# One load of attention values cut in two, and one spread of a bias row put three products later, in a fused decoder trunk on one core

## The chip, the cores and the metric

The kernel runs on one core of a Trainium2 chip. The metric is the device time of one execution in microseconds (us); the time of a kernel is the median of several executions. Beside it stands one execution that the hardware profiler recorded; its trace gives the span from the first to the last instruction and every row that is quoted below.

## The reference, cut to what matters

```python
mod = silu(c) @ w_ada + b_ada;  shift, scale, gate = split(mod, 3)
u = x * (1 + scale) + shift                       # 2048 x 1024
q, k, v, a_gate, p_in, p_gate, m_a, m_p = split(u @ w_in)
# 16 query heads of 64 on 2 key/value heads; window 128, blocks of 128 rows
logits = q_block @ [k_previous, k_own]^T / 8 + bias[head, distance]   # masked
probs  = softmax([logits, sink[head]])[..., :-1]
a = (probs @ [v_previous, v_own]) * silu(a_gate) @ w_attn_proj
p = (grouplinear(multiscale_pool(p_in)) * pool_scale * silu(p_gate)) @ w_pool_proj
y = ((sigmoid(m_a) * a + sigmoid(m_p) * p) @ w_out) * (1 + gate)
out = layer_norm(2**0.25 * x + y)
```

The eight query heads of one key/value head share its keys and values. The bias of a head depends on the distance between query and key alone, so a head's whole bias is one row of 384 numbers, read with a shift of one per query.

## The kernel before, in words

**The work.** The 2048 rows are taken in two chunks of 1024 (`s` = 0, 1), features in tiles of 128. All the large matrix products go through *quads* (class `Quad`): two 128-column weight tiles against two 512-row halves of a chunk, made as seven products after Strassen's and Winograd's scheme (B11, T1, T2, B21, T3, B22, T4). Each product is 12 matmuls of 128x128 by 512, because every operand is kept as a high and a low part and three of the four cross products are made. Weights of a quad arrive in tiles `W` and `A` (the last quarter), GpSimd (POOL) forms their sums and differences, ScalarE (ACT) and VectorE (DVE) split them into the parts `w_set`, TensorE (PE) multiplies.

**The order.** `plan` writes all products in one list, and `run` goes through it. `now[0]` is the number of the product that is made; `at(p, f)` hangs a function on product `p`, and `defer(n, f)` lets one run n products later. Each engine works through its own instructions in the order in which this walk emits them. Almost every DMA is issued by SyncE (SP, its queue SPq in the profile), so SP's order is a queue too: where one row waits (for data to be ready, for a buffer to be free, for an earlier transfer), all behind it wait. All operations are recorded by one helper, so nearly every row of the profile has line L56, and the tiles tell the rows apart.

**The overlay.** In each chunk a long phase (pools `o0` and `o1`) makes 13 quads one after the other and, between their matmuls, the attention of the same chunk (`overlay`, line 767). `beat` (line 940) is called after every third matmul and starts one attention step whenever enough credit has come together. There are 64 steps per chunk, each for two heads and one block of 128 queries; steps 0 to 31 are the first key/value group, 32 to 63 the second. In `step(n)` (line 871) PE makes the scores of block n into the one buffer `lg` (tiles `kk` and `qs`), the transposes of block n-2 (`pt`), and `values(n - 3)`, the product with the values (`pv<-pth,vv` and `pv<-ptl,vv`). DVE adds the bias `bt` to the scores and ACT makes the exponentials (tile `L`). PE takes its instructions in order, so when a step's operand is late, the large products behind it are late too.

**The values.** `load_v` (line 787) loads the values of one key/value group, 128 rows by 8 blocks of 128 numbers, into the tile `vv`, of which there is one. The second group's load is issued after step 34, the step that has made the last product with the first group's values, and its first reader, `values(32)`, is part of step 35; five calls of `beat` are skipped in between (`state[2] = 5`, line 955). For the second chunk the last block of the first chunk is loaded ahead of it with a DMA of its own. `values(32)` reads block 0 of `vv` in the first chunk, `values(33)` blocks 0 and 1, `values(34)` blocks 1 and 2.

**The bias.** `bias_rows` has written one row of 384 numbers per head to DRAM (`e_d`). `spread_bias(j, q)` (line 764) copies the rows of two heads to 128 places in the DRAM tile `e_rep` (384 KB), and `load_bias` (line 802) reads them back with a shift per partition into the tile `bt`, of which there is one; the load of the next two heads is issued in the last step of the present two. The eight spreads are hung on products: two early ones on ACT's queue, and j = 2 to 7 in the first overlay on SP's, at product `first + 10 * j - 17` (line 1443), with `first` the phase's first product. `e_rep` is one tile to the framework, so a spread waits until an earlier `bt` load has read it, though the rows are others.

**The query tiles.** The quads that make q store their result with two DMAs (`q_d<-q_hi`, `q_d<-q_lo`). The tiles `q_hi`, `q_lo`, `sig` and `px` share a ring of four buffers (tag `c`), so the third `q_hi` of a quad may be written when the store of its first one has landed.

Of the kernel before, what the change touches and what calls it, by code (L numbers as in the profile page):

```python
# [22 lines left out]
KT = D // P  # L23
CH = 512
NCH = S // CH
NB = CH // P
# [33 lines left out]
def kernel(  # L60
# [23 lines left out]
    pe, act, dve, pool, sp = (Ordered(tc, e) for e in (nc.tensor, nc.scalar, nc.vector, nc.gpsimd, nc.sync))  # L84
# [50 lines left out]
    v_d = dp.tile([2, P, 2, 2 * NB, P], F32, name="v_d")  # L135
# [11 lines left out]
    def as32(ap):  # L147
        return ap.bitcast(F32)
# [173 lines left out]
    def at(p, f):  # L322
        assert p >= now[0], (p, now[0])
        hooks.setdefault(int(p), []).append(f)
# [439 lines left out]
    def spread_bias(j, q):  # L764
        q.dma_start(e_rep[:, 2 * j : 2 * j + 2, :], e_d[2 * j : 2 * j + 2, :].partition_broadcast(P))

    def overlay(ph, s, n_slots):
# [19 lines left out]
        def load_v(kv):  # L787
            v = kvt["v"] = tp.tile([P, 2 * NB + s, P], F32R, tag="vv", bufs=1, name="vv")
            if s:
                sp.dma_start(as32(v[:, 0]), v_d[0, :, kv, 2 * NB - 1])  # L790
            sp.dma_start(as32(v[:, s:]), v_d[s, :, kv])

        def load_q(h):
            if h >= N // 2:
# [145 lines left out]
        def beat():  # L940
            n, credit, rest = state
            if rest:
                state[2] -= 1
                return
            state[1] += rate
            if state[1] >= 1 and n < N + 3:
                step(n)
                state[0] += 1
                state[1] -= 1
                if n == N // 2 - 1:  # L950
                    load_k(1)
                    state[2] = 8
                if n == N // 2 + 2:
                    load_v(1)
                    state[2] = 5
# [8 lines left out]
        load_q(0)  # L964
        load_bias(0)
        load_v(0)
        new_l(0)
        return beat, leave
# [34 lines left out]
    def input_sums(ph, first):  # L1003
        def load(u, k, at_c):
            sp.dma_start(u, xt[1, k].rearrange("p (h c) -> p h c", h=2)[:, :, at_c])

        def scale(u, k):
            act.activation(u, u, AF.Identity, bias=mod[:, k : k + 1], scale=mod[:, KT + k : KT + k + 1])

        for n in range(8):  # L1010
            steps(first, 1 + 11 * n, sums_job(ph, u1_d, n // 2, n % 2, load, scale))
# [424 lines left out]
    def middle(s):  # L1436
        def enter(ph, phase):
            first = phase["first"]
            beat, leave = overlay(ph, s, 4 * (phase["end"] - first))
            if s == 0:  # L1440
                input_sums(ph, first)
                for j in range(2, KT):
                    at(first + 10 * j - 17, lambda j=j: spread_bias(j, sp))
            return beat, leave

        return enter
# [120 lines left out]
```

## Time and profile before

| | us |
|---|---|
| median of 3 executions | 1715.49 |
| lowest and highest of them | 1715.05, 1715.85 |
| the profiled execution, its own time | 1721.38 |
| span of the profiled execution, first to last instruction | 1719.3 |

The profiled execution took 5.89 us more than the median, and 2.08 us of its time lie around the span. In rows of a timeline the columns are: start in us from the span's start, length in us, engine, line, operation, tile written <- tiles read, how many; in square brackets the time that the engine had been idle and what released it. SPq rows are the issue of a DMA, not its transfer; the transfer's end is called its landing. In rows that begin with a stretch (345.26:348.68) each engine has its busy time in the stretch and its number of instructions, then come the granted TensorE clock (1.00 is full), the mean busy share of the 16 DMA engines, and GB/s.

### The profile page before, as it was taken

Reading aid. Unit: us, or ns where it says so; the run is one execution under the profiler, and the core shown is the slowest. Engines: PE = TensorE matmul, PEld = TensorE weight load, DVE = VectorE, ACT = ScalarE, POOL = GpSimd, SP = SyncE. Lnnn points to the kernel's source line nnn. Section 1 sums busy time; section 2 is a strip of 40 time slices with the busy share of each in tenths; the row PEclk is TensorE's granted clock in tenths of the full one; section 3 lists DMA queues with packets and bytes.
Section 4 is the critical chain, followed back from the end, with each engine's and each line's share of the span. In section 5 each row is a group of like instructions: output and inputs, shape, how many; then the busy total and the mean of one; then the engine's idle time right before and its main releaser. Section 6 shows DMA issues by size and latency. Waiting matters only on the chain.

```text
span 1719.3 us, 24847 instructions
## 1 busy us (share of the span) xinstructions
PE 1672.1 (97%) x8112; PEld 1400.3 (81%) x8112; DVE 1274.5 (74%) x2295; ACT 945.4 (55%) x1815; POOL 590.5 (34%) x563
## 2 busy tenths in 40 slices
PE   9899999989999999999999999999999999999997
PEld 7678788878788888888888888888878888888886
DVE  5956787778756778658877888487886785778778
ACT  3644687767753436447777676433454443434552
POOL 3012455545553223323334243322243311113544
PEclk8999999999999999999999999999999999999999
DMA  9389666766547789873555544489978695778343
GB/s 355 120 285 301 204 213 228 244 214 201 190 162 228 254 281 316 285 249 119 183 178 188 180 145 154 160 268 325 336 260 290 199 331 182 259 261 295 147 147 122
DMA packets 236545, 389.50 MB, mean 227 GB/s; under 512 B 20840, under 2 KB 90240, under 8 KB 236288
## 3 DMA queue, kind: packets, MB, share of 16 engines
q1 hardware_dynamic: 235344, 386.55, 66.9%
q10 hardware_dynamic: 1040, 1.34, 0.3%
q8 instruction: 64, 1.05, 0.3%
q14 instruction: 65, 0.53, 0.1%
q0 software_dynamic: 32, 0.02, 0.0%
HBM read 243.63 MB, written 147.35 MB: 227 GB/s over the span
## 4 chain that ended last, share of the span: by engine, by line
PE 74%; DVE 10%; DMA 6%; ACT 5%; issue 4%; SPq 1%; POOL 0%; DVEq 0%; ACTq 0%; POOLq 0%
PE mm L56 46%; PE lg L56 12%; PE c L56 10%; PE pv L56 3%; PE pt L56 3%; DVE w_set L56 3%; DVE L L56 2%; ACT L L56 2%; ACT w_set L56 1%; DVE wide L56 1%; SPq L56 1%; DMA A<-in_win_dram 1%; ACT sig L56 1%; DMA qs<-q_d 1%; ACT q_hi L56 1%
## 5 line engine op out<-in xcount | busy, mean ns | idle before, releaser
L56 PE MATMUL mm<-set_B,w_set 128*128 128x512 f32 x2664 | 655.6, 393 | 1.5 <-DVE w_set L56 1.3
L56 PEld LDWEIGHTS mm<-set_B,w_set 128*128 128x128 f32 x2664 | 498.5, 189 | 105.5 <-DVE w_set L56 2.2
L56 PE MATMUL mm<-set_T,w_set 128*128 128x512 f32 x1896 | 470.4, 395 | 1.7 <-DVE set_T L56 0.9
L56 POOL TENSOR_TENSOR W<-W 128x512 f32<-128x512 f32 x185 | 267.2, 1454 | 568.3 <-DVE w_set L56 373.7
L56 PEld LDWEIGHTS mm<-set_T,w_set 128*128 128x128 f32 x1896 | 354.9, 191 | 75.4 <-DVE set_T L56 1.6
L56 DVE TENSOR_TENSOR w_set<-W,w_set 128x1024 fp32r<-128x1024 f32 x197 | 254.7, 1293 | 111.9 <-ACT w_set L56 101.9
L56 ACT CAST w_set<-W 128x1024 fp32r<-128x1024 f32 x222 | 232.2, 1047 | 92.8 <-PE mm L56 52.9
L56 ACT ACTIVATE L<-L 128x257 f32<-128x257 f32 (+3 forms) x384 | 191.2, 500 | 117.8 <-DVE L L56 117.2
L56 PE MATMUL lg<-set_T,w_set 128*128 128x512 f32 x828 | 201.1, 390 | 4.4 <-DVE set_T L56 2.3
L56 PE MATMUL c<-set_T,w_set 128*128 128x512 f32 x828 | 199.8, 390 | 0.0
L56 PEld LDWEIGHTS lg<-set_T,w_set 128*128 128x128 f32 x828 | 155.0, 188 | 37.9 <-DVE set_T L56 3.5
L56 PEld LDWEIGHTS c<-set_T,w_set 128*128 128x128 f32 x828 | 155.0, 188 | 32.1
L56 POOL TENSOR_TENSOR W<-W,A 128x512 f32<-128x512 f32 x41 | 56.2, 1371 | 283.6 <-DMA A<-in_win_dram 135.8
L56 DVE CUSTOM_DVE_ANT_0 L<-lg,bt,nsink 128x256 f32<-128x256 f32 (+1 forms) x256 | 111.0, 470 | 23.8 <-PE lg L56 17.5
L56 DVE TENSOR_TENSOR ptl<-pt,pth 128x512 fp32r<-128x512 f32 (+1 forms) x128 | 85.8, 670 | 30.3 <-ACT pth L56 29.3
L56 PEld LDWEIGHTS lg<-kk,qs 128*128 128x128 f32 x512 | 76.5, 189 | 36.7 <-DVE L L56 26.3
L56 PE MATMUL lg<-kk,qs 128*128 128x256 f32 (+1 forms) x512 | 83.6, 286 | 18.2 <-DVE L L56 17.6
L56 DVE TENSOR_SCALAR L<-L 128x256 f32<-128x256 f32 (+1 forms) x128 | 96.9, 757 | 4.5
L56 ACT ACTIVATE sig<-mm 128x512 f32<-128x512 f32 x76 | 45.5, 599 | 96.9 <-PE mm L56 94.7
L56 ACT CAST pth<-pt 128x512 fp32r<-128x512 f32 (+1 forms) x128 | 72.4, 565 | 24.6 <-PE pv L56 23.9
L56 POOL TENSOR_TENSOR w_set<-W,w_set 128x1024 fp32r<-128x1024 f32 x25 | 61.3, 2452 | 56.8 <-ACT w_set L56 31.1
L56 PE MATMUL pv<-pth,vv 128*128 128x256 f32 x248 | 75.4, 325 | 1.9 <-DMA vv<-v_d 1.9
(208 smaller groups left out, 1957.4 us busy)
## 6 DMA issues: line engine op xcount, KB each, us to landing
W<-in_win_dram SPq DMA_DIRECT2D x40, 512.0 KB, 5.8
qs<-q_d SPq DMA_DIRECT2D x128, 128.0 KB, 4.6
sums_d<-W SPq DMA_DIRECT2D x62, 256.0 KB, 4.2
W<-sums_d SPq DMA_DIRECT2D x31, 512.0 KB, 3.6
ain_d<-st SPq DMA_DIRECT2D x56, 256.0 KB, 3.6
A<-in_win_dram SPq DMA_DIRECT2D x42, 256.0 KB, 5.8
q_d<-q_hi SPq DMA_DIRECT2D x32, 256.0 KB, 3.9
q_d<-q_lo SPq DMA_DIRECT2D x32, 256.0 KB, 4.0
```

The costliest lines, as they stand in the source:

```text
L56: return lambda *args, **kw: self.tc.keep_in_program_order(op(*args, **kw))
```

## The change

The second group's values are loaded by two DMAs, blocks 0 and 1 (128 KB) first and blocks 2 to 7 (384 KB) right behind, in both chunks. The spread of the last bias rows (j = 7) hangs on product `first + 56` in place of `first + 53`. Nothing else differs; the numbers computed are the same.

```diff
         def load_v(kv):
             ...
-            sp.dma_start(as32(v[:, s:]), v_d[s, :, kv])
+            for a, b in ((0, 2), (2, 2 * NB)) if kv else ((0, 2 * NB),):
+                sp.dma_start(as32(v[:, s + a : s + b]), v_d[s, :, kv, a:b])
 ...
                 for j in range(2, KT):
-                    at(first + 10 * j - 17, lambda j=j: spread_bias(j, sp))
+                    at(first + (56 if j == KT - 1 else 10 * j - 17), lambda j=j: spread_bias(j, sp))
```

The order of the instructions changes on SP alone; PE, DVE, ACT and POOL have the same rows in the same order. At the second group's load in the first chunk, SP had this order (`qs` are query tiles, `px_d` a stored result, `A` and `sums_d` weights of the next quads):

```order
L56 DMA qs<-q_d 64x2x256 x2
L56 DMA vv<-v_d 128x1024
L56 DMA px_d<-px 128x512
L56 DMA A_3532<-in_win_dram 128x512
L56 DMA sums_d<-W 128x512
```

and has now

```order
L56 DMA qs<-q_d 64x2x256 x2
L56 DMA vv<-v_d 128x256
L56 DMA vv<-v_d 128x768
L56 DMA px_d<-px 128x512
L56 DMA A_3533<-in_win_dram 128x512
L56 DMA sums_d<-W 128x512
```

One row has become two; what stood behind it stands one row lower. The two instructions of `values(32)` wait for the first of the two loads now, and the second load is first waited for in `values(34)`.

At the last spread, SP had this order (`bt` is the bias of the sixth pair of heads, `q_hi` and `q_lo` a q quad's results, `A` the next weights, `ag` a gate):

```order
L56 DMA bt<-e_rep 128x2x256
L56 DMA e_rep<-e_d 128x768
L56 DMA q_d<-q_hi 128x512
L56 DMA q_d<-q_lo 128x512
L56 DMA A_3851<-wmix_d 128x512
L56 DMA ag<-ag_d 128x512
```

and has now, there and 14 rows further on,

```order
L56 DMA bt<-e_rep 128x2x256
L56 DMA q_d<-q_hi 128x512
L56 DMA q_d<-q_lo 128x512
L56 DMA A_3851<-wmix_d 128x512
L56 DMA ag<-ag_d 128x512
```

```order
L56 DMA ux<-in_xt_dram 128x2x256 x2
L56 DMA e_rep<-e_d 128x768
L56 DMA sums_d<-W 128x512
L56 DMA q_d<-q_hi 128x512
L56 DMA q_d<-q_lo 128x512
L56 DMA ain_d<-st 128x512
```

The spread has moved past 16 DMAs in 14 rows, the three pairs of q stores among them, and stands now between the load of `ux` (an input) and the store `sums_d` (a kept sum of weights), ahead of the quad's fourth pair of q stores.

## The prediction

> **What bounds the kernel now.** I read the page first, then the list of waits of TensorE over the whole run, then the timelines of TensorE, SyncE, ScalarE and GpSimd around the two places that the change touches, and last a table of stretches for the granted clock.
>
> ```profile
> PE 1672.1 (97%) x8112; PEld 1400.3 (81%) x8112; DVE 1274.5 (74%) x2295; ACT 945.4 (55%) x1815; POOL 590.5 (34%) x563
> PE 74%; DVE 10%; DMA 6%; ACT 5%; issue 4%; SPq 1%; POOL 0%; DVEq 0%; ACTq 0%; POOLq 0%
> ```
>
> TensorE is busy for 97% of the span and carries 74% of the chain that ended last. So a microsecond in which TensorE stands idle is worth about a microsecond of the whole, and there is little of it to be had. The list of waits (total, times, longest) names the two that matter here:
>
> ```profile
> PE lg L56 <- DVE L L56: 17.6, 17, 3.3
> PE pv L56 <- DMA vv<-v_d: 1.9, 1, 1.9
> ```
>
> The value product waits for its load once in the whole run, 1.9 us, and the longest wait of the scores is 3.3 us. TensorE's timeline has both; first the load:
>
> ```profile
> 342.68 0.60 PE L56 MATMUL pt<-ident,L 128*128 128x128 f32 x4
> 345.23 0.53 PE L56 MATMUL pv<-pth,vv 128*128 128x256 f32 x1 [1.95 <-DMA vv<-v_d]
> ...
> 345.77 1.48 PE L56 MATMUL mm<-set_B,w_set 128*128 128x512 f32 x3
> 347.05 3.69 PE L56 MATMUL mm<-set_T,w_set 128*128 128x512 f32 x12
> ...
> 351.98 3.58 PE L56 MATMUL mm<-set_T,w_set 128*128 128x512 f32 x15
> ```
>
> This is `values(32)` of the first chunk, so the change's first edit aims at this idle time. There is more to see: the 15 matmuls behind it take from 345.77 to 350.74, 4.97 us, and 15 of the same shape soon after take 3.58. The second place looks alike:
>
> ```profile
> 375.36 2.96 PE L56 MATMUL mm<-set_T,w_set 128*128 128x512 f32 x12
> 381.58 0.74 PE L56 MATMUL lg<-kk,qs 128*128 128x256 f32 x4 [3.26 <-DVE L L56]
> ...
> 383.05 5.09 PE L56 MATMUL mm<-set_T,w_set 128*128 128x512 f32 x15
> ```
>
> Again an idle time, and again 15 slow matmuls, 5.09 against 3.58 us. The table of stretches says why; its first pair is at the first place, its second at the second, and two pairs from earlier in the run follow:
>
> ```profile
> 341.85:345.26 3.41, 1.46 (x12) 1.18 (x10) 2.52 (x3) 1.20 (x2) 3.33 (x3) 1.00 1.04 393
> 345.26:348.68 3.42, 3.42 (x9) 2.82 (x10) 3.31 (x10) 2.97 (x9) 3.24 (x4) 0.50 1.02 367
> 379.40:382.81 3.41, 1.23 (x9) 1.16 (x10) 3.37 (x9) 2.81 (x8) 2.65 (x4) 1.00 1.07 408
> 382.81:386.22 3.41, 3.41 (x11) 2.73 (x10) 2.53 (x10) 3.36 (x10) 1.42 (x2) 0.50 0.77 235
> ```
>
> ```profile
> 178.00:181.42 3.42, 1.56 (x8) 0.96 (x7) 3.38 (x8) 1.28 (x4) 2.43 (x4) 1.00 0.76 281
> 181.42:184.84 3.42, 3.42 (x14) 3.13 (x15) 2.18 (x9) 2.82 (x10) 1.14 (x2) 0.50 0.44 132
> ```
>
> ```profile
> 65.37:68.79 3.42, 1.81 (x8) 1.54 (x9) 3.42 (x7) 3.21 (x6) 0.00 (x0) 1.00 0.20 77
> 68.79:72.20 3.41, 3.41 (x17) 2.77 (x16) 3.41 (x6) 0.00 (x0) 0.00 (x0) 1.00 0.88 202
> ```
>
> After a stretch with TensorE busy for 1.46, 1.23 or 1.56 of 3.41 us, the next stretch was granted half the clock; after one with 1.81 busy it kept the full clock. So an idle time of about 1.7 us inside one such stretch costs a second time, right behind itself. I call this the clock's share. It is the slow 15 matmuls: 4.97 - 3.58 = 1.39 us at the first place, 5.09 - 3.58 = 1.51 at the second; the most that 3.42 us at half the clock can cost is 1.71. I take 1.5 for each.
>
> **The first edit: values in two portions.** SyncE's timeline at the load:
>
> ```profile
> 336.43 1.36 SPq L56 DMA_DIRECT2D qs<-q_d  x2
> 337.89 0.61 SPq L56 DMA_DIRECT2D vv<-v_d  x1
> ...
> 339.60 0.33 SPq L56 DMA_DIRECT2D A<-in_win_dram  x1
> 341.56 0.32 SPq L56 DMA_DIRECT2D sums_d<-W  x1
> ```
>
> From issue to landing, the two `qs` loads took (shortest/median/longest)
>
> ```profile
> DMA to landing us min/median/max: 6.8/7.0/7.2
> ```
>
> and the `vv` load, alone in its answer,
>
> ```profile
> DMA to landing us min/median/max: 7.2/7.2/7.2
> ```
>
> The 512 KB landed at 337.89 + 7.2 = 345.1, 0.14 before TensorE went on. The second `qs` load (128 KB, issued 0.7 us before it) landed at about 344.0. These loads stand in one line behind each other: the stretch 341.85:345.26 has the DMA engines fully busy at 393 GB/s, so most of the 7.2 us is the queue in front, and cutting the load doesn't shorten that. What it takes off is the load's own tail, 345.1 - 344.0 = 1.1 us for 512 KB. A quarter of that is 0.3; the `qs` pair, 128 KB each, landed about 0.4 apart. So the first portion lands at 344.3 to 344.6, TensorE goes on 0.14 later, and of 1.95 us idle 0.5 to 0.8 is saved; I take 0.65. The bounds are 0 (lands as before) and 1.95 (lands by 343.28, where TensorE came free). The idle time that is left, 1.15 to 1.45, is under 1.7 wherever a stretch begins, so the clock's share goes too.
>
> But whether it was paid in the runs of the median hangs on where their stretches begin, which another execution need not share. Of 3.41 us of possible beginnings, those that hold 1.7 of a 1.95 us wait make 1.95 + 3.41 - 2 x 1.7 = 1.96: 0.57 of all. So 0.57 x 1.5 = 0.85 us on average, between 0 and 1.7.
>
> The second portion is first needed two steps later, behind 351.98, and has the same queue in front as the whole load had, so it lands near 345.1 with six microseconds to spare: no cost. The additional issue takes SyncE up to 0.61 us, in each chunk. In the second chunk no product waited for values, so nothing is gained there; nobody is shown waiting for SyncE at that point either, so I take 0 of a possible 0 to 0.6.
>
> **The second edit: the spread moved.** SyncE at the old place, then what it waited for between 361 and 376, then ScalarE:
>
> ```profile
> 368.44 0.38 SPq L56 DMA_DIRECT2D bt<-e_rep  x1
> 371.26 0.52 SPq L56 DMA_DIRECT2D e_rep<-e_d  x1
> 371.88 0.54 SPq L56 DMA_DIRECT2D q_d<-q_hi  x1
> ```
>
> ```profile
> SPq L56 <- DMA bt<-e_rep: 2.4, 1, 2.4
> ```
>
> ```profile
> 373.89 0.19 ACT L56 ACTIVATION_READ_ACCUMULATOR L<-L 128x1 f32 x1
> 376.44 0.60 ACT L56 ACTIVATE q_hi<-mm 128x512 fp32r<-128x512 f32 x1 [2.35 <-DMA q_d<-q_hi]
> ...
> 396.00 0.60 ACT L56 ACTIVATE sig<-mm 128x512 f32<-128x512 f32 x1
> ```
>
> The chain is: the spread may not overwrite `e_rep` while the `bt` load just issued reads it, so SyncE stands 2.4 us; the store of the quad's first `q_hi` stands behind it and is issued at 371.88; it lands about 4.5 us later, at 376.4; only then may ScalarE write the third `q_hi` into that buffer, 2.35 us after it came free; VectorE waits for that, then makes weights and, behind them, the bias step that frees `lg`; TensorE stands 3.26 us.
>
> With the spread gone from there the store is issued right after `bt`, at 368.44 + 0.38 + 0.05 = 368.9, 3.0 us earlier. Even with the same 4.5 us it lands at 373.4, before ScalarE is free (373.89 + 0.19 = 374.08). So all of ScalarE's 2.35 us goes, and what is late next is ScalarE and VectorE themselves: TensorE waits 3.26 - 2.35 = 0.9 us, too little for the clock. The bounds are 1.5 (some later link gives 0.85 back) and 3.26. The clock's share was nearly sure here (3.26 + 3.41 - 3.4 = 3.27 of 3.41, or 0.96): 1.45 us.
>
> At its new place the spread has no read to wait for, since `bt` landed ten microseconds earlier; its issue took 0.52 us here. Behind it stand a kept sum and the fourth pair of q stores; who waits for their buffers is a `sig` at 396.00. A q store issued by 387 lands, by the 4.5 us above, 4 us before that. So 0, with 0.5 as its upper end.
>
> **Sum.** 0.65 + 0.85 + 2.35 + 1.45 = 5.3 us less. Against the profiled execution's own 1721.38 that makes 1716.1; since both edits are costed as differences and TensorE bounds both, I carry them to the median: 1715.49 - 5.3 = 1710.2. The ends: 0.2 + 0 + 1.5 + 1.4 = 3.1 less (1712.4) and, with nearly everything won, 8 less (1707.5). A measurement of this kernel can tell about 0.2%, 3.4 us, from no change; the forecast lies outside that.
>
> **The rivals.**
>
> *The idle time goes, the clock's share stays* (chance 0.10). If the half clock came from something else than the idle time, 0.65 + 2.35 = 3.0 us remain: 1712.5, within 0.2%. Against it: three short-busy stretches above are each followed by half the clock, and the one with 1.81 busy is not. The Trainium skill, TensorE: Matmul & The Clock Gate, in HAM oscillation, gives the abstract rule as no idle gaps over about 3.4 us, which neither 1.95 nor 3.26 is; by it this rival holds. The trace disagrees with it, with half the clock right behind a gap of 1.95 us.
>
> *The first portion lands no earlier than the whole did* (0.10). If the DMA engine that is last takes the small pieces as slowly as the large, only the second edit counts: 2.35 + 1.45 = 3.8 less, 1711.7. The half microsecond between neighbours in the queue speaks against it.
>
> *The wait of the second place is replaced* (0.11). If VectorE's backlog, or the spread ahead of the stores at its new place, makes the same TensorE wait a few steps later, only the first edit counts: 0.65 + 0.85 = 1.5 less, 1714.0, no change that can be told. For it: VectorE is busy 3.37 of 3.41 us in 379.40:382.81. Against it: the 2.35 us are a wait for a landing and no work.
>
> *Slower: the additional transfer pushes the queue back* (0.04). Around the load SyncE issues only as earlier transfers land:
>
> ```profile
> SPq L56 <- DMA W<-in_win_dram: 2.1, 2, 1.6
> ```
>
> One transfer more moves `A` from 339.60 to, at the latest, the next row's 341.56: 1.96 us. Who waits for it is GpSimd, then ScalarE:
>
> ```profile
> 347.23 1.27 POOL L56 TENSOR_TENSOR W<-W,A 128x512 f32<-128x512 f32 x1
> ...
> 355.82 1.05 ACT L56 CAST w_set<-W 128x1024 fp32r<-128x1024 f32 x1
> ```
>
> If the next weights were late by that in both chunks, each would cost 1.96 and 1.71 for the clock, 7.3 together; with the first edit's gain lost and the second's 3.8 kept, that is 3.5 more, 1719.0. It decides from the point at which the sum ends after 355.82; it ends at 348.5, 7.3 us before, so it is unlikely.
>
> **How the numbers follow.** The forecast has 0.63, the rivals 0.35, and 0.02 is left for what I don't see. Below 1712.06 (faster by over 0.2%) lie most of the forecast and two thirds of the second rival: 0.67. Within 0.2% lie the first and third rivals, the rest of the second and the forecast's weak end: 0.28. Slower: 0.05. The range reaches from the forecast's strong end, 1707.5, past the third rival to 1714.3.
>
> **What would show it.** Right: in the changed kernel's trace the wait of `pv` for `vv` is 1.1 to 1.5 us, the wait of `q_hi` for its store is gone, the scores' longest wait is near 2 us or less and no longer at this place, and neither place is followed by half the clock. Wrong: a `vv` wait of still 1.9 us; a wait of `sig` or `q_hi` for a store behind the spread; half the clock without an idle time before it; POOL waiting for `A` at the next weights with TensorE idle behind it.

## The result and the profile after

| | before | after |
|---|---|---|
| median of 4 executions | 1715.67 | 1706.40 |
| lowest and highest | 1715.05, 1716.21 | 1704.28, 1708.46 |
| ratio, with its 95% interval | | 0.9936 [0.9917, 0.9955] |

By the medians that is 9.3 us less where 5.3 were forecast, and 1.1 us below the lower end of the range. The ratio is an estimate of its own and not the quotient of the two medians, which is 0.9946 here; where a difference below has an interval, both come from the ratio. A repeat with more executions (11 of the changed kernel, 34 of the kernel before, all on one chip) gave 1710.21 against 1717.02, ratio 0.9963 [0.9950, 0.9977]: 6.3 us less (3.9 to 8.6). Most of the distance between forecast and first result is therefore probably scatter, and the experiments show how large that is.

First the page of the changed kernel and two rows of its list of TensorE's waits (total, times, longest):

```profile
PE 1663.5 (97%) x8112; PEld 1393.1 (82%) x8112; DVE 1273.6 (75%) x2295; ACT 944.8 (55%) x1815; POOL 593.5 (35%) x563
```

```profile
PE lg L56 <- DVE L L56: 15.8, 17, 2.1
PE pv L56 <- DMA vv<-v_d: 0.2, 1, 0.2
```

The wait for the values is 0.2 where it was 1.9, and the scores' longest is 2.1 where it was 3.3. TensorE's timeline at the two places:

```profile
337.19 0.60 PE L56 MATMUL pt<-ident,L 128*128 128x128 f32 x4
337.99 0.36 PE L56 MATMUL pv<-pth,vv 128*128 128x256 f32 x1 [0.20 <-DMA vv<-v_d]
...
339.00 2.90 PE L56 MATMUL mm<-set_T,w_set 128*128 128x512 f32 x12
...
366.54 2.96 PE L56 MATMUL mm<-set_T,w_set 128*128 128x512 f32 x12
370.46 0.74 PE L56 MATMUL lg<-kk,qs 128*128 128x256 f32 x4 [0.96 <-DVE L L56]
...
371.81 3.59 PE L56 MATMUL mm<-set_T,w_set 128*128 128x512 f32 x15
```

The scores at the second place wait 0.96 us, as against 3.26; the 15 matmuls behind them take 3.59 us, not 5.09. Stretches at the two places (columns as in the table of before):

```profile
337.32:340.73 3.41, 3.21 (x18) 2.57 (x17) 3.38 (x4) 1.28 (x3) 3.41 (x3) 1.00 1.06 403
340.73:344.14 3.41, 3.41 (x23) 3.04 (x22) 3.23 (x13) 3.14 (x9) 3.13 (x5) 1.00 0.97 327
368.03:371.45 3.42, 2.46 (x14) 1.77 (x13) 3.37 (x10) 2.58 (x8) 2.65 (x3) 1.00 1.04 392
371.45:374.86 3.41, 3.41 (x19) 2.88 (x18) 2.50 (x11) 3.36 (x10) 1.26 (x2) 1.00 0.86 219
```

Both places keep the full clock. Last, SyncE's timeline:

```profile
331.15 1.26 SPq L56 DMA_DIRECT2D qs<-q_d  x2
332.50 1.02 SPq L56 DMA_DIRECT2D vv<-v_d  x2
...
359.61 0.38 SPq L56 DMA_DIRECT2D bt<-e_rep  x1
360.08 0.42 SPq L56 DMA_DIRECT2D q_d<-q_hi  x1
...
370.68 1.58 SPq L56 DMA_DIRECT2D ux<-in_xt_dram  x2
372.31 0.61 SPq L56 DMA_DIRECT2D e_rep<-e_d  x1
```

The store of `q_hi` is issued 0.47 us behind `bt` (it was 3.44), and the spread stands behind `ux` and waits for nothing.

**Where the time went between these two traces.** Equal rows, start in after minus start in before: the transposes ahead of the first place 337.19 - 342.68 = -5.5 us; the large product behind it 339.00 - 347.05 = -8.1; the one ahead of the second place 366.54 - 375.36 = -8.8; the scores there 370.46 - 381.58 = -11.1; then 5.09 - 3.59 = 1.5 more by the clock; the spans differ by 13.1. So 7.1 us came at the two places (3.3 and 3.8), and 5.5 were there before either, where the two programs are the same. The last 0.5 came behind them, again where the half clock fell: before was granted 0.50 from 471.56 to 474.97, behind a wait of 2.14 us for scores, and after kept the full clock behind the same wait of 2.12 us; after was granted 0.50 from 1039.75 to 1043.16, behind a wait of 1.75 us, and before kept the full clock behind the same wait of 1.74. The first scores of the overlay (first row before, second after) show the head start already, and stretches of the first 60 us show a part of it:

```profile
L56 PE MATMUL lg<-kk,qs x28: 225/283/477, 167.9 to 197.6; 128*128 128x256 f32 x24, 128*128 128x128 f32 x4
```

```profile
L56 PE MATMUL lg<-kk,qs x32: 275/282/386, 164.1 to 197.2; 128*128 128x256 f32 x28, 128*128 128x128 f32 x4
```

```profile
0.00:60.00 60.00, 54.96 (x253) 45.62 (x254) 37.73 (x67) 27.25 (x44) 13.58 (x40) 0.86 0.72 268
27.80:41.50 13.70, 13.02 (x42) 11.09 (x42) 6.28 (x11) 4.76 (x9) 0.00 (x0) 0.50 1.04 404
```

```profile
0.00:60.00 60.00, 53.91 (x264) 43.58 (x265) 42.19 (x75) 29.73 (x48) 14.68 (x40) 0.91 0.71 268
```

The recorded execution of before ran 13.7 us of its head at half the clock; that of after had 0.91 on average in the same 60 us, against 0.86. The change isn't in the head, so this belongs to these two executions; a second trace of the changed kernel has 13.7 us of its head at half the clock too (28.10 to 41.76).

### The profile page after: what moved, and what is told of

Same layout as the page of the kernel before. It is cut to its first block, busy times and chain, and to the rows that moved or that the text cites. A ratio compares the mean times of both kernels' runs of the same rounds, so it can differ in the third digit from the quotient of the medians.

```text
span 1706.2 us, 24850 instructions
## 1 busy us (share of the span) xinstructions
PE 1663.5 (97%) x8112; PEld 1393.1 (82%) x8112; DVE 1273.6 (75%) x2295; ACT 944.8 (55%) x1815; POOL 593.5 (35%) x563
## 4 chain that ended last, share of the span: by engine, by line
PE 69%; DVE 9%; DMA 6%; ACT 5%; issue 4%; POOL 1%; SPq 0%; DVEq 0%; ACTq 0%; POOLq 0%
PE mm L56 43%; PE lg L56 12%; PE c L56 9%; DVE w_set L56 3%; PE pv L56 3%; PE pt L56 3%; DVE L L56 2%; ACT L L56 2%; ACT w_set L56 1%; DVE wide L56 1%; ACT sig L56 1%; DVE p L56 1%; DMA q_d<-q_hi 1%; DMA ux<-in_wout_dram 1%; ACT q_hi L56 1%
## 5 line engine op out<-in xcount | busy, mean ns | idle before, releaser
L56 PE MATMUL pt<-ident,L 128*128 128x128 f32 x496 | 76.4, 275 | 0.0
```

The lines of the kernel that those rows point to most:

```text
L56: return lambda *args, **kw: self.tc.keep_in_program_order(op(*args, **kw))
```

## The experiments

The theory: two waits on transfers are gone, and with them the half clock behind them, worth about 5 us together; what the first result showed beyond that is scatter. The rivals: the change does more than the two places show; or the half clock has another cause than the idle time; or the spread gained by where it now stands and not by what it no longer waits for.

### The same kernel again, each edit alone, and both

The control is the kernel before, unchanged.

> The kernel before, unchanged, as a control. Theory A: the change is worth what the two places show in the traces, about 7 us (values 3.3, spread 3.8), and the rest of the 9.3 us between the medians is execution to execution variation in the head of the kernel, in the queue of transfers and in where the half-clock stretches fall. Then this control scatters by 1 to 3 us around the kernel before, its trace again has the values' wait (1 to 2 us) and the scores' wait of 3.2 us at the spread, and its first 325 us differ from the first trace's by up to 5 us. Theory B: the change has a further real effect of 2 us or more somewhere else. Then the control scatters by under 1 us.

Measured: 1715.64 (1712.70 to 1720.32, 12 executions) against 1717.02 (1711.12 to 1723.21, 34), ratio 0.9993 [0.9980, 1.0007]. Executions of one program on one chip lie up to 12 us apart. Its trace shows the same two waits as that of before, and then something that was not in the forecast. TensorE at the second place, and stretches at both places (the first pair the first place):

```profile
369.10 2.96 PE L56 MATMUL mm<-set_T,w_set 128*128 128x512 f32 x12
375.35 0.74 PE L56 MATMUL lg<-kk,qs 128*128 128x256 f32 x4 [3.29 <-DVE L L56]
...
376.71 3.58 PE L56 MATMUL mm<-set_T,w_set 128*128 128x512 f32 x15
```

```profile
336.32:339.73 3.41, 1.35 (x10) 1.09 (x9) 3.35 (x4) 0.86 (x2) 3.41 (x3) 1.00 1.05 401
339.73:343.15 3.42, 3.42 (x9) 2.64 (x8) 2.50 (x9) 3.30 (x9) 2.42 (x3) 0.50 0.92 340
370.45:373.87 3.42, 1.61 (x7) 0.95 (x6) 2.76 (x4) 1.99 (x4) 0.73 (x1) 1.00 1.08 366
373.87:377.28 3.41, 1.93 (x13) 1.78 (x14) 3.33 (x11) 2.81 (x9) 2.08 (x4) 1.00 1.05 387
```

A wait of 3.29 us costs no clock when a boundary cuts it into 1.81 and 1.48: the 15 matmuls behind it take 3.58 us. The same wait was followed by half the clock in the trace of before.

The load in two portions alone:

```diff
-            sp.dma_start(as32(v[:, s:]), v_d[s, :, kv])
+            for a, b in ((0, 2), (2, 2 * NB)) if kv else ((0, 2 * NB),):
+                sp.dma_start(as32(v[:, s + a : s + b]), v_d[s, :, kv, a:b])
```

> The values in two portions alone, the spread at its old place. Theory A: the values' wait falls from about 1.9 to 0.2 to 0.8 us and the half clock behind it goes, 2 to 3.4 us less than before; the scores' wait of 3.2 us and its half clock stay. Theory B (a further effect that belongs to the values, for instance in the second chunk): 5 us or more less, with a second place after 900 us where time is won.

Measured: 1714.42 (12 executions), ratio 0.9988 [0.9975, 1.0000]: between 0 and 4.3 us less, not to be told from the control. In its trace the product waits 0.38 us for the values; the scores at the second place wait 3.28 and again keep the clock:

```profile
368.31:371.72 3.41, 1.55 (x7) 0.94 (x5) 2.81 (x4) 1.98 (x4) 0.78 (x1) 1.00 1.09 335
371.72:375.14 3.42, 1.99 (x13) 1.84 (x14) 3.34 (x13) 2.82 (x9) 2.03 (x4) 1.00 1.05 394
```

The spread moved alone:

```diff
-                    at(first + 10 * j - 17, lambda j=j: spread_bias(j, sp))
+                    at(first + (56 if j == KT - 1 else 10 * j - 17), lambda j=j: spread_bias(j, sp))
```

> The spread moved alone, the values in one load. Theory A: the scores' wait falls from 3.2 to 0.9 us and the half clock behind it goes, 3.8 us less than before; the values' wait stays at 1 to 2 us. Theory B (a further effect that belongs to the spread): 6 us or more less, with time won at some other place than these 5 us.

Measured: 1711.52 (1707.40 to 1718.12, 12 executions), ratio 0.9963 [0.9949, 0.9977]: 6.3 us less (3.9 to 8.8). The scores wait 0.97 at the second place; the product waits 1.04 for a load that is still in one piece. The size is that of Theory B, but the trace shows no other place where time was won: from the scores at the second place to the last instruction it has 1338.1 us, the trace of before 1337.7 and that of the control 1336.8.

Both, which is the changed kernel:

> The changed kernel again, beside the others on one chip. Theory A: 7 us less than before, 6 to 8.5, the sum of the two edits alone within 1.5 us. Theory B: 9 us or more less again, more than the two edits alone add up to.

Measured: 1710.21 (1706.69 to 1714.46, 11 executions), 0.9963 [0.9950, 0.9977]. Its trace has waits of 0.20 and 0.97 and no half clock at either place, yet its span is 1709.2 us, 3.0 more than that of after. The spread carries most of the gain; what the two portions are worth is smaller than these runs can tell.

### Is it the read that the spread waits for, or its place?

The spread of the last rows at its old place, into a DRAM tile of its own, so that it doesn't wait for the read of other rows:

```diff
+    e_last = dp.tile([P, 2, ET], F32, name="e_last")
...
+        dst = e_last if j == KT - 1 else e_rep[:, 2 * j : 2 * j + 2, :]
+        q.dma_start(dst, e_d[2 * j : 2 * j + 2, :].partition_broadcast(P))
```

(`load_bias` reads the last rows from there.)

> The kernel before, with the spread at its old place but the last bias rows in a DRAM tile of their own, so that it need not wait until the bias load just ahead has read the shared tile. Theory A (the wait for the read, 2.4 us on SyncE's queue, is what holds the q store): SyncE no longer stands there, the store is issued about 1.0 us after the bias load instead of 3.4, ScalarE's wait for the store is under 0.3 us, TensorE's wait for the scores falls from 3.3 to 0.9 to 1.2 us, 3.5 us less than before. Theory B (the 384 KB that lie ahead of the store on the DMA engines hold it): the scores' wait stays over 2 us, at most 1.5 us less than before.

Measured: 1712.70 (1708.03 to 1713.79, 12 executions) against 1715.12 (34), ratio 0.9972 [0.9957, 0.9986]. SyncE's timeline, ScalarE's, and TensorE's:

```profile
361.97 0.38 SPq L56 DMA_DIRECT2D bt<-e_rep  x1
362.40 0.52 SPq L56 DMA_DIRECT2D e_last<-e_d  x1
363.01 0.54 SPq L56 DMA_DIRECT2D q_d<-q_hi  x1
```

```profile
367.43 0.19 ACT L56 ACTIVATION_READ_ACCUMULATOR L<-L 128x1 f32 x1
368.31 0.60 ACT L56 ACTIVATE q_hi<-mm 128x512 fp32r<-128x512 f32 x1 [0.70 <-DMA q_d<-q_hi]
```

```profile
368.89 2.96 PE L56 MATMUL mm<-set_T,w_set 128*128 128x512 f32 x12
373.47 0.74 PE L56 MATMUL lg<-kk,qs 128*128 128x256 f32 x4 [1.61 <-DVE L L56]
```

The store goes out 1.04 us behind `bt`, not 3.44, yet ScalarE still waits 0.70 us for it, since the store lands behind the 384 KB of the spread (5.2 us from issue to landing, against 3.7 in after). The scores' wait falls from 3.26 to 1.61, and to 0.96 only when the spread is gone from there. About 1.65 of 2.3 us was thus the wait for the read, and the rest is the spread's own transfer ahead of the store. The result lies between the two expectations: the read is the larger part, and neither part is the whole.

The spread four products earlier than before instead of three later, with one load of the values:

```diff
-                    at(first + 10 * j - 17, lambda j=j: spread_bias(j, sp))
+                    at(first + (49 if j == KT - 1 else 10 * j - 17), lambda j=j: spread_bias(j, sp))
```

> The kernel before with the last spread 4 products earlier in place of 3 later, so that it stands 9 rows ahead of the bias load whose read it had to wait for; the values in one load. Theory A (what counts is only that the spread no longer stands between that load and the q stores): as with the spread moved later, the scores' wait falls to 0.9 to 1.0 us, 3.5 to 6 us less than before. Theory B (the new place itself, later in the phase, won something): less than half of that, or a wait at the new place, since around it SyncE issues only as earlier transfers land.

Measured: 1709.57 (1708.21 to 1712.91, 12 executions) against 1715.54 (23), ratio 0.9966 [0.9952, 0.9980]; the scores' wait is 0.97, as with the spread three products later. So the new place itself does nothing; being away from the `bt` load and the `q_hi` store is what counts.

### The order of the portions

```diff
-            for a, b in ((0, 2), (2, 2 * NB)) if kv else ((0, 2 * NB),):
+            for a, b in ((2, 2 * NB), (0, 2)) if kv else ((0, 2 * NB),):
```

> The changed kernel with the two portions of the values in the other order: blocks 2 to 7 first, blocks 0 and 1 behind them. Theory A (the first reader waits for what is in front of its blocks, its own load's tail among it): the values' wait is that of one load again, 1 to 2 us, the second place is as in the changed kernel. Theory B (the number of transfers, or something other than the order of the blocks, shortened the wait): the wait stays under 0.5 us.

Measured: 1709.45 (1707.95 to 1711.77, 7 executions), 0.9963 [0.9944, 0.9982], the same as the changed kernel. The wait was 1.12 us, longer than 0.20, but traces of kernels with the portions in the right order have 0.20, 0.38, 0.20, 1.12 and 0.99 (the last two from runs below), so the wait of one trace settles nothing here. The landings say more. The first portion, with the right order, landed 5.4, 5.9, 6.2, 5.8 and 6.2 us after its issue; the whole load, in the five traces that have it in one piece and no added matmuls, after 7.2, 7.1, 6.7, 6.9 and 6.5. With the order changed, the large portion went out at 330.91 and the small one at 331.8, and by this row (shortest, median, longest) the small one landed 6.4 us later, 7.3 after the large one's issue:

```profile
DMA to landing us min/median/max: 6.4/6.7/7.0
```

So the order does bring the needed blocks in about 1 us earlier, as Theory A has it. How much of that shows in TensorE's wait hangs on when TensorE comes free, and in the time of these executions it doesn't show.

### The clock's share: the idle time filled

If idle time sets the clock, matmuls that compute nothing needed, put into it, keep the clock without removing any wait. On the kernel before, into the buffer of the transposes ahead of the scores of four steps, and five more ahead of `values(32)`:

```diff
+        def fill(acc, n):
+            t = sets["B11"][:, 0, 0, :]
+            for _ in range(n):
+                mm(acc, t[:, 0:P], t, start=True, stop=True, skip_group_check=True)
...
+            early, idle = None, {(0, 3): 4, (0, 42): 8, (0, 60): 4, (1, 60): 3}.get((s, n))
+            if idle:
+                early = ps.tile([P, 2, 2, P], F32, tag="pt", bufs=1, name="pt")
```

> The kernel before, with products that nobody reads set into TensorE's five longest waits of the two overlays (5 ahead of the values' wait; 8, 4, 4 and 3 ahead of four waits for the scores), so that the waits end when they ended before but the part without work is shorter. Theory A (an idle time of over about 1.8 us in one stretch of 3.41 us costs half the clock in the next): no half-clock stretch from 120 us to the end in this trace, and 2 to 4 us less than before, though no wait was removed. Theory B (the half clock has another cause): half-clock stretches stay and the time is the same or up to 1 us longer.

Measured: 1721.08 (12 executions), ratio 1.0035 [1.0020, 1.0049], slower. TensorE at the second place:

```profile
371.48 2.96 PE L56 MATMUL mm<-set_T,w_set 128*128 128x512 f32 x12
378.02 3.78 PE L56 MATMUL pt<-set_B 128*128 128x512 f32 x8 [3.58 <-DVE ptl L56]
381.60 1.06 PE L56 MATMUL lg<-kk,qs 128*128 128x256 f32 x4
```

The fills waited themselves, for VectorE to read the buffer they were to write. The idle time stayed, and the fills came on top, at half the clock (3.78 us for 8). It tells nothing about the theory.

The changed kernel with such fills at three steps:

> The changed kernel, with such products ahead of the three waits of over 1.7 us that it has left in the overlays (4, 4 and 3). Theory A: no half clock from 120 us on, 1 to 2.5 us less than the changed kernel, so 7 to 9 us less than before. Theory B: as the changed kernel, 6 to 7 us less than before, or slightly longer.

Measured: 1715.79 (12 executions), 0.9997 [0.9984, 1.0011]: what the change had gained is gone. The flaw is the same: TensorE waits three times, 7.6 us in all, for VectorE to read that buffer.

Mended: on the kernel before, into the buffer `pv` of the step's own value product, which is free at that point:

```diff
+            room = bank("pv") if n - 3 in xs else None
+            fill(n, room, {(0, 3): 4, (0, 42): 8, (0, 60): 4, (1, 60): 4})
             lg = scores(n) if n < N else None
...
+            fill(n, room, {(0, 32): 5})
```

> Again the kernel before with products that nobody reads set into TensorE's five longest waits of the overlays (5 ahead of the values' wait; 8, 4, 4 and 4 ahead of four waits for the scores), now into the free one of the two pv buffers, which doesn't wait for VectorE; in the first attempt they went into the pt buffer, stood behind the wait themselves and made it longer. Theory A (too long an idle time in one stretch of 3.41 us costs half the clock in the next): the idle parts fall to 0.6 to 1.5 us, the waits end where they ended, no half-clock stretch from 120 us on, 2 to 5 us less than before though no wait was removed. Theory B (the half clock has another cause): half-clock stretches stay in the overlays and the time is the same or up to 1 us longer.

Measured: median 1712.66 of twelve executions against 1715.54 (23), ratio 0.9979 [0.9964, 0.9994]; eleven of them took 1709.25 to 1717.85, and the twelfth 2318.79, which I can't explain. TensorE at the two places, and long stretches:

```profile
334.87 1.39 PE L56 MATMUL pv<-set_B 128*128 128x512 f32 x5
...
367.67 2.00 PE L56 MATMUL pv<-set_B 128*128 128x512 f32 x8
371.18 0.74 PE L56 MATMUL lg<-kk,qs 128*128 128x256 f32 x4 [1.51 <-DVE L L56]
...
372.54 3.59 PE L56 MATMUL mm<-set_T,w_set 128*128 128x512 f32 x15
```

```profile
55.00:500.00 445.00, 428.08 (x2307) 363.91 (x2306) 328.64 (x812) 299.06 (x675) 194.18 (x203) 1.00 0.69 224
500.00:1060.00 560.00, 552.81 (x2785) 466.23 (x2784) 421.19 (x860) 335.57 (x706) 191.74 (x187) 1.00 0.64 213
```

The edit takes away no transfer and no dependency that anything waits for, and yet the time falls by 3.6 us (1.0 to 6.2), with the granted clock at 1.00 throughout both stretches. That is the clock's share by itself, at those of the five places where an execution pays it; in the trace of before, the stretch from 102.91 to 500 us had 0.98:

```profile
102.91:500.00 397.09, 384.46 (x2065) 328.10 (x2065) 288.84 (x723) 272.05 (x630) 175.14 (x189) 0.98 0.69 223
```

The changed kernel with the mended fills, four each at steps 3 and 60 of the first chunk and 60 of the second:

> The changed kernel with such products in the free pv buffer ahead of the three waits of over 1.7 us that it has left in the overlays (4 each). Theory A: no half clock from 120 us on, 1 to 2.5 us less than the changed kernel, so 7 to 9 us less than before. Theory B: as the changed kernel, 6 to 7 us less than before, or slightly longer.

Measured: 1707.24 (1703.60 to 1710.26, 6 executions) against 1715.54, ratio 0.9944 [0.9923, 0.9965], 9.6 us less (6.0 to 13.2). That is the largest difference of the experiments, but its interval overlaps that of the changed kernel without the fills (3.9 to 8.6), so what the fills add to the change isn't shown by the times. The trace has the full clock in both of these stretches:

```profile
78.50:500.00 421.50, 412.30 (x2236) 352.07 (x2235) 305.55 (x776) 285.87 (x653) 194.72 (x203) 1.00 0.71 232
500.00:1060.00 560.00, 552.99 (x2791) 466.52 (x2790) 424.11 (x866) 338.86 (x712) 191.87 (x186) 1.00 0.64 211
```

### The first portion from another queue

The last version again, with the first portion issued by ScalarE, outside SyncE's line:

```diff
-                sp.dma_start(as32(v[:, s + a : s + b]), v_d[s, :, kv, a:b])
+                (act if kv and a == 0 else sp).dma_start(as32(v[:, s + a : s + b]), v_d[s, :, kv, a:b])
```

> The changed kernel with the unread products of the last experiment ahead of its three long waits, and the first portion of the second group's values issued by ScalarE, whose transfers have a line of their own, in place of SyncE. Theory A (what is left of the values' wait, 0.2 to 1.1 us in the traces, is the line of transfers that SyncE has issued before, not the 128 KB themselves): the first portion lands 2 to 4 us after its issue in place of 5.4 to 6.2, and the wait is gone in the first chunk; 0 to 1 us less than the kernel without it, 7.5 to 10 us less than before. Theory B (the DMA engines are full whoever issues): it lands after 5 us or more and the wait stays.

Measured: 1710.75 (1707.66 to 1715.53, 10 executions) against 1715.53 (15), ratio 0.9977 [0.9963, 0.9991], 3.9 us less than before (1.5 to 6.3). That falls short of Theory A's 7.5 to 10, though the interval still just touches that of the version before it. The timeline of ScalarE, the landings of the two portions (shortest, median, longest), TensorE, and the stretch behind:

```profile
335.10 0.36 ACTq L56 DMA_DIRECT2D vv<-v_d  x1
```

```profile
DMA to landing us min/median/max: 6.9/7.1/7.2
```

```profile
342.40 0.55 PE L56 MATMUL pv<-pth,vv 128*128 128x256 f32 x1 [2.79 <-DMA vv<-v_d]
```

```profile
342.22:345.63 3.41, 3.23 (x9) 2.68 (x10) 2.60 (x10) 2.59 (x8) 2.60 (x3) 0.50 0.79 285
```

ScalarE came to it only 0.63 us after SyncE had issued the other portion (at 334.47), and it landed 7.2 us after its own issue, where it took 5.4 to 6.2 from SyncE's queue. Theory A's 2 to 4 us fell. But the small portion now went out behind the 384 KB and not ahead of them, so this run doesn't tell what the other queue alone would do.

## Why the prediction was right and wrong

**Both mechanisms held in the traces; in the times only the second edit's shows.** The wait for the store and the scores' wait at the second place went as worked out: what was left is 0.96 to 0.97 us in after, in the repeat and with the spread moved alone (forecast 0.9), where it was 3.26 to 3.29. ScalarE doesn't wait there any more, and nothing behind the spread waits for it. Most of the values' time to landing is what stands in front, as forecast; in after the small portion landed at 332.50 + 5.4 = 337.9 and the rest, issued at 333.1, at 338.8, by this row:

```profile
DMA to landing us min/median/max: 5.4/5.5/5.7
```

That is 0.9 earlier than the rest, and 1.0 earlier on average over the five traces each (5.9 us after the issue against 6.9), where the forecast had 0.5 to 0.8. The wait of 0.20 in after is shorter than the 1.1 to 1.5 that the prediction named as its sign, in part by luck: of the 1.8 us between 7.2 and 5.4, half came with that execution and not with the cut, since the rest of the load landed 6.3 us after the first issue there. In the five traces the rest landed after 6.3 to 7.2 us, as the whole load does: no cost, as forecast.

**The step that failed is the last one,** "The ends: 0.2 + 0 + 1.5 + 1.4 = 3.1 less (1712.4) and, with nearly everything won, 8 less (1707.5)". The range has its lower end, 1707.5, from there. (The 0.2 stands nowhere else; the bound worked out for that term was 0.) It put the scatter of the two medians at nothing, as if they were known to a microsecond, because three executions lay within 0.8; even the 3.4 us that the prediction names as what a measurement can tell were not added. The 34 executions of the unchanged kernel beside the repeat lie between 1711 and 1723 (standard deviation 2.9), so two means of four executions differ by about 2.9 x sqrt(2/4) = 2 us without any change. The recorded execution's 1721.38, 5.9 above the median, had said so, and was set aside. By the repeat the difference is 6.3 us (3.9 to 8.6): the forecast of 5.3 lies within it. That the first result fell below the range was most likely the luck of eight executions.

**Term by term.** *The values' wait, 0.65:* the traces with one load and no fills have 1.95, 2.06, 1.04, 1.46 and 0.35, mean 1.4; those with two portions 0.20, 0.38, 0.20, 1.12 and 0.99, mean 0.6. That is 0.8 on average, near the forecast, though the two groups overlap; the 1.75 between before and after is partly luck. *Its clock, 0.85:* of the five with one load only the two longest waits, 1.95 and 2.06, are long enough; both were followed by half the clock. Two in five times 1.5 is 0.6. *The spread, 2.35:* 2.3. *Its clock, 1.45 at a chance of 0.96:* Of three traces with the old spread at its place and no fills, one had half the clock behind it and two had none. The limit of 1.7 us was a little low and isn't sharp: 1.80 us idle in a stretch (1.61 busy) and 1.86 (1.55 busy, in the run with the two portions alone) were followed by the full clock, 1.86 (1.56 busy, in before at 178 us) and 1.74 (1.67 busy, in the run with the portions in the other order) by half:

```profile
1036.49:1039.90 3.41, 1.67 (x10) 1.10 (x9) 3.37 (x9) 2.38 (x7) 1.47 (x2) 1.00 0.78 231
1039.90:1043.31 3.41, 3.41 (x14) 3.02 (x14) 2.54 (x10) 2.48 (x7) 0.19 (x1) 0.50 0.20 74
```

Over the steps of all 14 traces, from 20 us on and with the full clock, none with less than 1.74 us idle was followed by half the clock and every one with more than 1.90 was; of 16 in between, 7 were. With 1.74 to 1.90 in place of 1.7, the prediction's own working gives a chance of 0.84 to 0.94, so 1.3 to 1.4 us; one in three traces is less, but three are few, and between 0.5 and 1.4 us stays open. The sum by these is 4.2 to 5.1.

The times with the spread moved are larger than its terms: 6.3 us (3.9 to 8.8) three products later and 5.8 (3.4 to 8.2) four products earlier, where the traces show 2.3 and at most 1.5 at that place. The 3.8 lies at the lower end of both intervals, and no trace shows where more would come from.

**The rivals.** That the clock's share has another cause than the idle time is refuted by the fills, which won 3.6 us with every wait's cause left in place, and by the steps of the 14 traces. The Trainium skill, TensorE: Matmul & The Clock Gate, in HAM oscillation, gives as the abstract rule that there be no idle gaps over about 3.4 us. It isn't enough here: half the clock followed waits of 1.95 and 2.06 us. That the first portion lands no earlier is refuted by the landings (5.4 to 6.2 us against 6.5 to 7.2), and that the second place's wait is replaced shows in no trace. Of the slower one nothing was seen either: between 325 and 400 us TensorE waits in after for the values and for scores alone, 2.2 us in all, and not for weights.

**What stays open.** How much time the two portions are worth by themselves ([0.9975, 1.0000]), which by the scatter of 2.9 us would take some hundred executions to tell; whether the moved spread wins more than the 3.8 us that its place shows; and why the head's half clock differs between executions. A second buffer for the values, which would have let the load start earlier, wasn't tried.

## What to carry to other kernels

Before a forecast of a few tenths of a per cent, look for what one program's own executions differ by, the recorded one among them, and put it into the range; three that agree are not a scatter. Where a queue's row overwrites a tile that has just been read, look at what stands behind it in the queue: here SyncE's wait of 2.4 us for a read of other rows, with the spread's own transfer, came out at TensorE as 2.3. Idle time on the bounding engine can cost twice, and filling it with idle matmuls is worth a try, if their target is free at that moment.

## What the runs showed of the hardware

- Behind the head, the half clock comes in steps of 3.41 us whose beginnings lie elsewhere in each trace, so a wait of 3.26 us cost a clock's share in one and a wait of 3.29 none in another. The border lies between 1.74 and 1.90 us idle in one step.
- Its price is 1.4 to 1.5 us at the two places (15 matmuls took 4.97 and 5.09 us, not 3.58), and filling five such places of the kernel before took 3.6 us off it.
- The head of the program is where executions differ: the first score of the overlay started at 167.9 us in before and 164.1 in after, and between 160.5 and 168.7 in the 14 traces, with nothing changed ahead of it.
- With the DMA engines fully busy (393 and 403 GB/s in the stretches of before and after), the values' 512 KB landed 6.5 to 7.2 us after their issue, 128 KB issued first after 5.4 to 6.2, and 128 KB from ScalarE's queue, behind 384 KB from SyncE's, after 7.2.
